# Start of the split-weight buffers inside a 128-byte line, in a two-block transformer kernel on one core

## The chip, the cores and the metric

The kernel runs on one core of one Trainium2 chip. The metric is the device time of one execution in microseconds, and a kernel is told by the median of its runs.

## The reference

Two blocks of two layers each are computed for one sequence of 256 tokens with 1024 features, in float32. The first block mixes a gated linear recurrence with latent attention and then sends every token to two of sixteen experts; the second has a gated recurrence, a chunked attention and wide MLPs. What takes the time is matrix products with weights that are each used once:

```
proj = h @ w_in                                   # 1024 x 4768, per layer of block 1
he = jax.nn.silu(t @ w_gate[e]) * (t @ w_up[e])   # 16 experts, 1024 x 512
y = y + combine[:, e:e + 1] * (he @ w_down[e])
z = hn @ w_in                                     # block 2, recurrence, 1024 x 2816
sqrelu_mlp: jnp.square(jax.nn.relu(hn @ w1)) @ w2 # 1024 x 4096 x 1024, twice
```

## The kernel before

Activations lie with features on the 128 partitions and the 256 tokens along the free dimension. Weights arrive in pieces of 1 MB (128 partitions x 2048 floats) in a ring of five buffers `raw`, loaded by SyncE's queue in the order in which `weights()` (L399) is called. `parts_of()` (L429) splits each half of a piece, 1024 floats in a partition, into a rounded part and a rest: ScalarE writes `whi` (L444), VectorE subtracts and writes `wlo` (L445). The pool `wsp` has three buffers of each, taken in turn by the counter `turn`; the recurrent layer adds two more of each (pool `wse`, `EXTRA`).

Each product in float32 is then made of three matmuls in `mm3()` (L456): high by high (L459), low by high (L460) and high by low (L461). Every matmul has a stationary operand, which a weight load (PEld) brings into the array, and a moving operand, which streams through it. The names of a matmul in the trace stand as out<-moving,stationary.

- In linears (`linear_gen`, L475) a slice of 128 columns of `whi` or `wlo` is stationary, 512 bytes in a partition, and the activations move, 256 tokens, 1024 bytes. The tiles are `h_hi`/`h_lo`, `a_hi`/`a_lo` (the MLP's hidden layer), `xc`, `mg`, `oa`, `ob`, `hq`, `oo`.
- In token-major linears (`linear_tok_gen`, L529; the values of the first block, keys and values of the second) a slice of `h` is stationary and 256 columns of `whi`/`wlo` move.
- In the experts (`project` and `down` in `moe`) a slice of `xg` or `hT` is stationary and 512 columns of `whi`/`wlo` move.

The scheduling is by program order on each engine, with semaphores between them. [...]

The layout that the program is built with: `whi` begins at 101632, 105728 and 109824 bytes in a partition, `wlo` at 113920, 118016 and 122112. All six are multiples of 128, and a slice's start adds a multiple of 512. `h_hi` begins at 44224, `h_lo` at 52416, `xc_hi` and `a_hi` at 134720, that is, at 64 past a multiple of 128; `xg`, `hT` and the other expert tiles begin at multiples of 128. Small unused tiles (`shift`) put them there. The attention's probabilities `p`, which are stationary in the transposes of L1179, begin at 32 or 96 past a multiple of 128 in the mixers and at 0 or 64 past one in the second block's attention.

The one place outside the weights where an operand begins off such a boundary is the convolution of the recurrent layer (L1601), which reads `xr[:, j:j + T]` for j = 1, 2, 3, at 4, 8 and 12 bytes past a tile's start.

Of the kernel before, what the change touches and what calls it, by code (L numbers as in the profile page):

```python
# [9 lines left out]
F32R = mybir.dt.float32r  # L10
# [7 lines left out]
D, T, P = 1024, 256, 128  # L18
# [4 lines left out]
CONV = 1024  # L23
# [159 lines left out]
def program(tc, A, out, dbg=None):  # L183
    nc = tc.nc
    from contextlib import ExitStack, nullcontext
    with ExitStack() as st:
# [217 lines left out]
        def weights(ap, nk, nn):  # L404

            if READY and not OWN:
                return READY.pop(0)
            raw = PRE.pop(0) if PRE and not OWN else None
            if raw is None:
                raw = OWN[0].tile([P, RING], F32, tag="own", name="own") if OWN else room()  # L410
                with tc.issue_after(LOADS[0].ins) if LOADS else nullcontext():
                    nc.sync.dma_start(raw[:, :nk * nn], ap[:, :nk * nn])
            if GATE:
                with ExitStack() as es:
                    for g in GATE.pop():
                        es.enter_context(tc.issue_after(g.ins))
                    return parts_of(raw, nk, nn)
            return parts_of(raw, nk, nn)

        EXTRA, turn = [None, 0], [-1]  # L420
# [5 lines left out]

        DEFER = []

        def parts_of(raw, nk, nn):  # L429
            per_ = max(1, CONV // nn)  # L430
            parts = []
            for k0 in range(0, nk, per_):
                n = min(per_, nk - k0) * nn
                src = raw[k0 // per_] if isinstance(raw, list) else raw[:, k0 * nn:k0 * nn + n]
                if OWN:
                    hl = (OWN[1].tile([P, 2, CONV], F32R, tag="e0", name="own_w") if k0 == 0 else
                          OWN[2].tile([P, 2, CONV], F32R, tag="cn", name="own_w"))
                    hi, lo = hl[:, 0], hl[:, 1]
                else:
                    turn[0] = (turn[0] + 1) % (3 + EXTRA[1])  # L440
                    p_ = wsp if turn[0] < 3 else EXTRA[0]
                    hi = p_.tile([P, CONV], F32R, tag="whi", name="whi")
                    lo = p_.tile([P, CONV], F32R, tag="wlo", name="wlo")
                nc.scalar.copy(hi[:, :n], src)  # L444
                low = lambda lo=lo, hi=hi, src=src, n=n: nc.vector.tensor_sub(lo[:, :n], src, hi[:, :n].bitcast(F32))  # L445
                if k0 and DEFER:
                    DEFER.append(low)
                else:
                    low()
                parts.append((hi, lo))  # L450

            def w(k, c, n):
                i, o = k // per_, k % per_ * nn + c
                return [t[:, o:o + n] for t in parts[i]]
            return w
# [336 lines left out]
        def first_linear(pcs, nxt, mw, mx, ma, evac):  # L792
# [42 lines left out]
            for i, raw in enumerate(raws):  # L835
                w = parts_of(raw, 8, 2 * P)
                ps = bank(("hg", "at")[i // 2], "ps_f").rearrange("p (c t) -> p c t", c=2)
                pss += [ps[:, 0], ps[:, 1]]
                for n, (k, c) in enumerate([(k, c) for k in range(8) for c in range(2)] if i == 0 else
                                           [(k, c) for c in range(2) for k in range(8)]):  # L840
                    wh, wl = w(k, c * P, P)
                    nc.tensor.matmul(ps[:, c], wh, y[0][:, k, :], start=n == 0, stop=False, skip_group_check=True)
                    nc.tensor.matmul(ps[:, c], wh, y[1][k], start=False, stop=False, skip_group_check=True)
                    nc.tensor.matmul(ps[:, c], wl, y[0][:, k, :], start=False, stop=k == 7, skip_group_check=True)
                    if n % 8 == 7:
                        m = 2 * i + n // 8
                        ada_fill(SHIFT[m])
                        if m == SHIFT_DONE[0]:
                            shift_done()
                        if m == SHIFT_DONE[1]:  # L850
                            shift_products()
                        if m == NEXT:
                            ready(nxt)
# [1047 lines left out]
```

## Time and profile before

| | us |
|---|---|
| runs: median, lowest, highest of 3 | 1828.7, 1824.86, 1834.02 |
| profiled execution, its own time | 1828.03 |
| span of its instructions | 1826.3 |
| TensorE busy (matmul) in the span | 1750.9 |
| VectorE busy | 1465.8 |
| ScalarE busy | 1130.6 |

The profiled execution lies 0.7 us below the median; 1.7 us of its time lie outside the span. In the stretches named below, 58 to 285 us and 605 to 860 us are the mixers of the first block's layers, 285 to 605 us and 860 to 1168 us their experts, 1168 to 1306 us the recurrent layer, 1306 to 1500 us the first MLP, 1500 to 1650 us the attention and 1650 to 1826 us the second MLP. Matmuls are pipelined, so the length that the profile gives one (280 ns) is longer than the distance to the next; where a stream runs without a wait, its pace is read from the starts.

### The profile page before, as it was taken

The numbers are of one execution on the slowest core, as the hardware profiler recorded it, in microseconds if no ns is written. First come the engines' busy times: TensorE is split into PE (matmuls) and PEld (weight loads), VectorE is DVE, ScalarE is ACT, GpSimd is POOL, SyncE is SP. The second block draws the span as 40 slices with busy tenths as digits, with TensorE's granted clock in tenths as the row PEclk, the third lists the DMA queues.
The fourth block names the chain that finished last, engine by engine and source line by source line (L and its number), as shares of the span: only waits on it lengthen the run. The fifth ranks groups of instructions, "written<-read, shape, count | busy, mean of one in ns | idle before, by whom it ended". The sixth has DMA issues, their size and how long they took to land. (4 is left out here: it accounts for less than half of the span.)

```text
span 1826.3 us, 31669 instructions
## 1 busy us (share of the span) xinstructions
PE 1750.9 (96%) x12430; PEld 1551.3 (85%) x12430; DVE 1465.8 (80%) x2514; ACT 1130.6 (62%) x1758; POOL 39.2 (2%) x40
## 2 busy tenths in 40 slices
PE   7999998999999899998999999999999999999999
PEld 5887897888878797897888887798899998889999
DVE  4887897999998677898998999797897666667754
ACT  3754546877777556545877777578555446546642
POOL 0000000000000000000000000000000002100000
PEclk9999998999999899999999999899999999999999
DMA  9565797797999456688697899657687764456552
GB/s 352 216 246 226 275 347 283 283 347 278 353 344 344 146 209 251 245 323 346 250 345 303 326 354 357 236 203 262 215 323 280 273 248 148 173 189 258 203 194 85
DMA packets 71727, 485.62 MB, mean 266 GB/s; under 512 B 8720, under 2 KB 10896, under 8 KB 14352
## 3 DMA queue, kind: packets, MB, share of 16 engines
q1 hardware_dynamic: 70992, 483.21, 71.0%
q8 instruction: 101, 1.65, 0.4%
q14 instruction: 58, 0.48, 0.1%
q10 hardware_dynamic: 576, 0.27, 0.1%
HBM read 482.41 MB, written 1.05 MB: 265 GB/s over the span
## 5 line engine op out<-in xcount | busy, mean ns | idle before, releaser
L445 DVE TENSOR_TENSOR wlo<-raw,whi 128x1024 fp32r<-128x1024 f32 (+1 forms) x628 | 752.9, 1210 | 151.7 <-ACT whi L444 136.6
L444 ACT CAST whi<-raw 128x1024 fp32r<-128x1024 f32 (+1 forms) x628 | 649.8, 1041 | 272.8 <-PE ps_mm L460 162.7
L459 PE MATMUL ps_mm<-h_hi,whi 128*128 128x256 f32 x1168 | 330.5, 286 | 6.8 <-ACT h_hi L656 4.2
L461 PE MATMUL ps_mm<-h_hi,wlo 128*128 128x256 f32 x1168 | 328.1, 283 | 1.5 <-DVE wlo L445 1.4
L460 PE MATMUL ps_mm<-h_lo,whi 128*128 128x256 f32 x1168 | 329.1, 283 | 0.0
L459 PEld LDWEIGHTS ps_mm<-h_hi,whi 128*128 128x128 f32 x1168 | 222.5, 192 | 12.6 <-ACT h_hi L656 5.9
L461 PEld LDWEIGHTS ps_mm<-h_hi,wlo 128*128 128x128 f32 x1168 | 222.7, 191 | 4.8 <-DVE wlo L445 3.7
L460 PEld LDWEIGHTS ps_mm<-h_lo,whi 128*128 128x128 f32 x1168 | 223.1, 191 | 2.1 <-issue 1.4
L460 PE MATMUL ps_e<-wlo,xg 128*128 128x512 f32 x512 | 202.4, 395 | 2.6 <-DVE wlo L445 2.3
L459 PE MATMUL ps_e<-whi,xg 128*128 128x512 f32 x512 | 202.7, 396 | 1.2 <-ACT whi L444 1.1
L461 PE MATMUL ps_e<-whi,xg 128*128 128x512 f32 x512 | 200.2, 391 | 0.0
L459 PE MATMUL ps_mm<-a_hi,whi 128*128 128x256 f32 x512 | 142.4, 278 | 0.0
L461 PE MATMUL ps_mm<-a_hi,wlo 128*128 128x256 f32 x512 | 142.1, 278 | 0.0
L460 PE MATMUL ps_mm<-a_lo,whi 128*128 128x256 f32 x512 | 142.1, 278 | 0.0
L305 DVE SCALAR_TENSOR_TENSOR raw<-raw,cb 128x1024 f32<-128x1024 f32 x112 | 135.6, 1216 | 1.5 <-DMA raw<-in_ada_dram 1.4
L460 PEld LDWEIGHTS ps_e<-wlo,xg 128*128 128x128 f32 x512 | 96.2, 188 | 26.8 <-DVE wlo L445 8.5
L459 PEld LDWEIGHTS ps_e<-whi,xg 128*128 128x128 f32 x512 | 96.2, 188 | 20.8 <-ACT whi L444 1.9
L461 PEld LDWEIGHTS ps_e<-whi,xg 128*128 128x128 f32 x512 | 96.1, 188 | 18.6
L460 PE MATMUL py<-wlo,hT 128*128 128x512 f32 x256 | 101.0, 394 | 0.0
L461 PE MATMUL py<-whi,hT 128*128 128x512 f32 x256 | 99.8, 390 | 0.0
L459 PE MATMUL py<-whi,hT 128*128 128x512 f32 x256 | 99.2, 390 | 0.0
L461 PEld LDWEIGHTS ps_mm<-a_hi,wlo 128*128 128x128 f32 x512 | 96.2, 188 | 0.0
(694 smaller groups left out, 3476.5 us busy)
## 6 DMA issues: line engine op xcount, KB each, us to landing
raw<-in_ada_dram SPq DMA_DIRECT2D x104, 1024.0 KB, 5.9
raw<-in_mw_dram SPq DMA_DIRECT2D x64, 1024.0 KB, 4.9
raw<-in_w_up_dram SPq DMA_DIRECT2D x56, 1024.0 KB, 4.9
raw<-in_w_down_dram SPq DMA_DIRECT2D x56, 1024.0 KB, 4.9
raw<-in_w_gate_dram SPq DMA_DIRECT2D x44, 1024.0 KB, 4.8
raw<-in_win_dram SPq DMA_DIRECT2D x34, 1024.0 KB, 5.0
more<-in_w_gate_dram SPq DMA_DIRECT2D x12, 1024.0 KB, 5.1
raw<-in_lwin_dram SPq DMA_DIRECT2D x11, 1024.0 KB, 5.9
```

Source lines behind the costliest of these rows:

```text
L305: nc.vector.scalar_tensor_tensor(w, w, 1.0, cb, op0=OP.mult, op1=OP.mult, accum_out=mod[:, m:m + 1])
L444: nc.scalar.copy(hi[:, :n], src)
L445: low = lambda lo=lo, hi=hi, src=src, n=n: nc.vector.tensor_sub(lo[:, :n], src, hi[:, :n].bitcast(F32))
L459: nc.tensor.matmul(ps, ah, bh, start=start, stop=False)
L460: nc.tensor.matmul(ps, ah, bl, start=False, stop=False)
L461: nc.tensor.matmul(ps, al, bh, start=False, stop=stop)
```

## The change

Every buffer of `whi` and `wlo` is made 128 bytes longer, and 4096 of its 4224 bytes are used, from a start that depends on the buffer: 30, 31 or 2 floats (120, 124 or 8 bytes) where the piece is not 512 columns wide, and 0 where it is.

```diff
+        LINE = (30, 31, 2)
+
         def parts_of(raw, nk, nn):
...
                     p_ = wsp if turn[0] < 3 else EXTRA[0]
-                    hi = p_.tile([P, CONV], F32R, tag="whi", name="whi")
-                    lo = p_.tile([P, CONV], F32R, tag="wlo", name="wlo")
+                    o = LINE[turn[0] % 3] if nn != 512 else 0
+                    hi = p_.tile([P, CONV + 32], F32R, tag="whi", name="whi")[:, o:o + CONV]
+                    lo = p_.tile([P, CONV + 32], F32R, tag="wlo", name="wlo")[:, o:o + CONV]
```

The instructions, their order on every engine and their waits are the same in both programs. Of the matmuls of `mm3`, 6150 of 256 columns get a stationary operand that begins at 120, 124 or 8 past a multiple of 128, and 576 of 256 columns (and 24 of 512) such a moving operand. The 2304 of the experts, and 384 of the mixers' output projections, whose pieces are 512 columns wide too, keep multiples of 128. All tiles behind `wsp` move by 768 bytes, six times 128; `h_hi`, `h_lo` and the ring stay. The six buffers now lie 4224 bytes apart instead of 4096.

## Rows read from the trace of the kernel before

**Rows 1.** Page, part 1: the span and TensorE's busy time.

```profile
span 1826.3 us, 31669 instructions
...
PE 1750.9 (96%) x12430; PEld 1551.3 (85%) x12430; DVE 1465.8 (80%) x2514; ACT 1130.6 (62%) x1758; POOL 39.2 (2%) x40
```

**Rows 2.** Stretches: a mixer, experts, recurrent layer, attention; engines' busy us (instructions), clock, DMA.

```profile
58.00:285.00 227.00, 220.07 (x1745) 195.81 (x1743) 192.51 (x487) 126.68 (x259) 5.91 (x6) 0.98 0.71 267
285.00:605.00 320.00, 306.35 (x1440) 251.67 (x1441) 287.73 (x343) 239.95 (x275) 2.31 (x2) 0.97 0.83 312
1168.00:1306.00 138.00, 131.15 (x1170) 120.80 (x1163) 117.19 (x205) 96.78 (x162) 0.70 (x1) 0.99 0.67 246
1500.00:1650.00 150.00, 143.86 (x1223) 123.68 (x1223) 99.04 (x243) 85.50 (x204) 19.54 (x17) 0.99 0.48 180
```

**Rows 3.** Stretches of 100 us inside the two MLPs, columns as in rows 2.

```profile
1385.00:1485.00 100.00, 100.00 (x852) 100.00 (x851) 66.77 (x92) 43.38 (x54) 0.00 (x0) 1.00 0.73 267
1655.00:1755.00 100.00, 100.00 (x885) 100.00 (x884) 69.23 (x102) 58.41 (x99) 0.00 (x0) 1.00 0.57 197
```

**Rows 4.** Timeline of PE: first and last matmul followed 116 to 119 ns later.

```profile
58.79 0.28 PE L459 MATMUL ps_mt<-whi,h_hi 128*128 128x256 f32 x1
...
1653.94 0.28 PE L461 MATMUL ps_mm<-h_hi,wlo 128*128 128x256 f32 x1
```

**Rows 5.** Timeline of PE: first and last matmul followed 113 to 115 ns later.

```profile
69.89 0.28 PE L460 MATMUL ps_mt<-wlo,h_hi 128*128 128x256 f32 x1
...
1822.13 0.28 PE L460 MATMUL ps_mm<-a_lo,whi 128*128 128x256 f32 x1
```

**Rows 6.** Timeline of PE, experts: start, length, line, out<-moving,stationary; nine matmuls from first to last.

```profile
472.24 0.39 PE L461 MATMUL ps_e<-whi,xg 128*128 128x512 f32 x1
...
474.28 0.39 PE L461 MATMUL ps_e<-whi,xg 128*128 128x512 f32 x1
```

**Rows 7.** Groups of the page, part 5: the two halves of the split.

```profile
L445 DVE TENSOR_TENSOR wlo<-raw,whi 128x1024 fp32r<-128x1024 f32 (+1 forms) x628 | 752.9, 1210 | 151.7 <-ACT whi L444 136.6
L444 ACT CAST whi<-raw 128x1024 fp32r<-128x1024 f32 (+1 forms) x628 | 649.8, 1041 | 272.8 <-PE ps_mm L460 162.7
```

**Rows 8.** Groups by form on VectorE: 256 floats read at odd starts, and at even ones.

```profile
L1601 DVE SCALAR_TENSOR_TENSOR y<-xr,c_cols,y 128x256 f32<-128x256 f32 x33 | 14.8, 479 | 0.0
...
L654 DVE SCALAR_TENSOR_TENSOR nt<-xT,gain,rs 128x256 f32<-128x256 f32 x16 | 7.1, 479 | 1.7 <-ACT rs L1759 1.7
```

**Rows 9.** Timeline of PE: four transposes of `p` in a mixer and four in the attention.

```profile
203.51 0.60 PE L1179 MATMUL ps_pt<-c_ident,p 128*128 128x128 f32 x4
...
1599.55 0.60 PE L1179 MATMUL ps_pt<-c_ident,p 128*128 128x128 f32 x4
```

**Rows 10.** Timeline of PE, first MLP: two stretches of nine matmuls around a short gap.

```profile
1366.13 0.28 PE L459 MATMUL ps_mm<-h_hi,whi 128*128 128x256 f32 x1
...
1367.19 0.28 PE L459 MATMUL ps_mm<-h_hi,whi 128*128 128x256 f32 x1
...
1367.43 0.32 PE L461 MATMUL ps_mm<-h_hi,wlo 128*128 128x256 f32 x1
1367.58 0.28 PE L459 MATMUL ps_mm<-h_hi,whi 128*128 128x256 f32 x1
...
1367.93 0.28 PE L459 MATMUL ps_mm<-h_hi,whi 128*128 128x256 f32 x1
...
1368.95 0.28 PE L459 MATMUL ps_mm<-h_hi,whi 128*128 128x256 f32 x1
```

**Rows 11.** Timeline of PE, recurrent layer: six matmuls before and after a new moving tile.

```profile
1228.17 0.28 PE L459 MATMUL ps_mm<-h_hi,whi 128*128 128x256 f32 x1
...
1228.85 0.28 PE L459 MATMUL ps_bd<-xc_hi,whi 128*128 128x256 f32 x1
...
1229.56 0.28 PE L459 MATMUL ps_bd<-xc_hi,whi 128*128 128x256 f32 x1
```

## The prediction

> **What bounds the kernel now.** The profiled execution took 1828.03 us, 0.7 below the median of 1828.7, and its instructions span 1826.3; the sum below is made against 1828.0. I read the page's busy times first: TensorE is busy 1750.9 us of the span, 96%, VectorE 80% and ScalarE 62% [rows 1]. By stretch it is no different: 220 of 227 us in a mixer, 306 of 320 in the experts, 131 of 138 in the recurrent layer, 144 of 150 in the attention [rows 2]. So time is won or lost in the pace at which matmuls follow each other.
>
> That pace is the second thing to read. [...] Among the 6922 pairs of matmuls of `mm3` with 256 columns that follow each other in the whole trace, 3289 are 116 to 119 ns apart [rows 4], 3211 are 113 to 115 ns apart [rows 5], and 422 are further apart or wait. Of the slow ones 1142 lie in the first MLP, 1 in the second, 1096 in the two mixers, 433 in the recurrent layer, 615 in the attention and 2 in the experts' stretches. In the experts' quiet stretches nine matmuls of 512 columns take 2.04 us, 226.7 ns each, which is the fast level for twice the columns [rows 6].
>
> **What the change does, part by part.** It moves no instruction and no wait; it moves addresses. Four things could cost or give.
>
> The writers. ScalarE's and VectorE's split, 1.04 and 1.21 us [rows 7], now write to starts 8 or 12 bytes past a multiple of 16. The nearest rows are the convolution's 33 operations, which read 256 floats at 4, 8 and 12 bytes past a tile's start: 479 ns, the same as 16 operations of that form at even starts [rows 8]. I take 0. Were each of the 628 a per cent slower, VectorE would lose 7.5 us in all, and in the linears, where the odd starts are, it is idle for a third of the time (67 us busy of 100 in the first MLP [rows 3]); so the bounds on the path are 0 and 7.5 us.
>
> The weight load by itself. A slice of 512 bytes that starts at 120, 124 or 8 lies in one 128-byte line more than before. The nearest rows are the transposes, whose stationary `p` starts at 32 or 96 past a multiple of 128 in the mixers, and at 0 or 64 past one in the attention: four of them take 0.60 us in both places [rows 9]. Those starts are still multiples of 32, so this says little of 8 and 124, but a load by itself shows no price. I take 0, with the slow level as the upper bound (below).
>
> The pace. This is the term. What is it that tells a fast stream from a slow one? The level holds for hundreds of matmuls and survives from slice to slice and buffer to buffer. In this layout all buffers look alike to TensorE, since all of them, and all slices, start at a multiple of 128. It changes where the stream is disturbed: in the first MLP nine matmuls take 1.06 us (117.8 ns), then one comes 0.15 us after its predecessor instead of 0.12, and soon nine take 1.02 us (113.3) [rows 10]. And once it changes with no wait at all, at the place where the moving tile goes from `h` to `xc`, another address: six matmuls take 0.68 us before it and 0.71 after [rows 11]. I read this as two streams, the load of the next weights and the running matmul, which go through their lines of memory side by side; in one relation of phase they get into each other's way by 4.4 ns in a matmul, in the other they don't, and the relation lasts until something shifts it. A start that is one or two floats away from the boundary shifts the load's crossings against the matmul's; and since the three buffers have three different starts, the relation is set anew every 8 slices (24 matmuls), so that a slow stretch of 850 matmuls at one phase [rows 3] is no longer possible. 6150 matmuls get such a start. My forecast is that the linears then run at the fast level nearly everywhere.
>
> The price, if they do: the first MLP gives 1142 x 4.4 ns = 5.0 us, all on the path, as TensorE has no idle time there. Mixers, recurrent layer and attention hold 1096 + 433 + 615 = 2144 slow pairs, 9.4 us; VectorE is busy 193 of 227 us in a mixer and 117 of 138 in the recurrent layer [rows 2], so part of what TensorE gains there it will spend waiting for the split, and I count four fifths, 7.5 us. Together 12.5 us: 1828.0 - 12.5 = 1815.5, I say 1816. Its own range is 1811 (some of the experts' uneven stretches profit too) to 1822 (half of it).
>
> The experts. They keep multiples of 128, at the fast level for the most part [rows 6]. But the buffers lie 4224 apart instead of 4096, so two of three change by 128 against a multiple of 256, and the change of pace in [rows 11] was between two tiles that are both 64 past a multiple of 128. Bounds: 0, and 2304 x 8.8 ns = 20 us lost if all of them fell to the slow level. I take 0, as nothing else here points to 256, and put the bound into the range.
>
> [...]
>
> **The rivals.** First, no change: the level is set by the moment at which a stream restarts after a wait, whatever the addresses are. For it speaks that both levels occur at the same starts, thousands of times each [rows 4, 5], and that the change of pace comes with a gap [rows 10]; against it [rows 11], where no gap is. Then the shares stay as they are, with the luck of the two MLPs: one that turns slow costs 1510 x 4.4 = 6.6 us, one that turns fast gives 5.0. That is 1828, between 1822 and 1835, which is also about how far the three runs lie apart.
>
> Second, slower: the line that each shifted load touches in addition is one more place for the two streams to meet, and it is there in every phase. The nearest price for a meeting is the slow level itself: if the 3211 fast pairs become slow, 3211 x 4.4 = 14 us are lost, four fifths to all of it on the path, 1839 to 1842. It decides against the change from 9.1 us on, that is, 1.5 ns in each of the 6150 shifted matmuls. For it speaks that the starts before are all multiples of 32, the second MLP runs 1510 pairs at the fast level with them, and none starts in the middle of 16 bytes; against it that a load at 32 or 96 shows no price [rows 9]. [...]
>
> Third, a larger gain: with no meeting of any kind the pace could fall to that of the transposes, of which four take 0.60 us with the 0.28 that the last one lasts, 0.11 us from start to start [rows 9, 10]. Some 4 ns below the fast level on 6150 matmuls are 25 us more, 1791. Nothing in 6500 pairs of linears lies below 113 ns, so this gets little.
>
> **How the numbers follow.** Forecast (fast level) 46%, no change 30%, slower 19%, larger gain 5%. A measurement of this kernel tells a difference from none at about 0.5%, 9.1 us. Of the forecast's 46 about 40 end beyond that, with the larger gain 45; of the slower rival's 19 and the unlucky end of no change 22 in all; 33 stay within. The range must hold forecast and no change, 1811 to 1835; it reaches a little further on both sides, 1808 to 1838, and leaves out the larger gain and most of the slower rival, 5 and 13%.
>
> **What would show it.** In the profile after: the two stretches of 100 us in the MLPs both with 880 matmuls or more, and the pairs at 116 to 119 ns reduced from 3289 to some hundreds; the split still 1.04 and 1.21 us; the experts' nine matmuls still in 2.04 us. The forecast is wrong if both levels keep their shares (the first rival), if the share at 113 to 115 shrinks or a third, slower level appears (the second), or if the pace improves and the time doesn't, in which case VectorE's split has become what TensorE waits for.

## The result, and the profile after

The changed kernel takes 1844.34 us, the median of its runs (1841.75 to 1846.5), against 1826.88 for the kernel before, measured beside it: a ratio of 1.0082 with a 95% interval of 1.006 to 1.0104. It is slower; forecast were 1816 us and a range up to 1838. The profiled execution took 1844.61 us. The page after, part 1, answers to [rows 1]; TensorE has gained 21 us of busy time, the other engines next to nothing:

```profile
span 1842.8 us, 31669 instructions
...
PE 1772.0 (96%) x12430; PEld 1568.1 (85%) x12430; DVE 1468.4 (80%) x2514; ACT 1130.4 (61%) x1758; POOL 39.2 (2%) x40
```

The lines of the code lie four further: `mm3` at L463 to L465, the split at L448 and L449. The split groups (page, part 5, as [rows 7]) cost what they did, at starts inside 16 bytes too:

```profile
L449 DVE TENSOR_TENSOR wlo<-raw,whi 128x1024 fp32r<-128x1024 f32 (+1 forms) x628 | 754.0, 1210 | 160.9 <-ACT whi L448 156.9
L448 ACT CAST whi<-raw 128x1024 fp32r<-128x1024 f32 (+1 forms) x628 | 649.6, 1040 | 286.4 <-PE ps_mm L464 171.1
```

Stretches after, columns as in [rows 2]: the first layer's experts, and 100 us in each MLP, as far from the MLP's first matmul as in [rows 3]:

```profile
284.00:607.00 323.00, 311.27 (x1439) 253.68 (x1439) 289.04 (x343) 239.54 (x275) 2.30 (x2) 0.96 0.82 309
...
1393.00:1493.00 100.00, 100.00 (x849) 100.00 (x848) 67.46 (x92) 43.25 (x55) 0.00 (x0) 1.00 0.74 268
1664.00:1764.00 100.00, 100.00 (x846) 100.00 (x845) 66.74 (x100) 56.70 (x98) 0.00 (x0) 1.00 0.54 191
```

Neither MLP runs at 880 or more: the second fell from 885 to 846 matmuls in 100 us at the same clock, and the first stayed where it was. The two levels of before (113.3 and 117.8 ns) are gone: taken 24 at a time (as many as one buffer serves), those of the second MLP with h moving have means of 117.8 to 119.4 ns, where each group had 113.3 before. A timeline of PE there (start, length, line) has 24 matmuls from the first to the last row in 2.85 us, 118.8 ns each; single distances differ (0.13, then 0.11):

```profile
1699.73 0.28 PE L463 MATMUL ps_mm<-h_hi,whi 128*128 128x256 f32 x1
...
1701.15 0.28 PE L463 MATMUL ps_mm<-h_hi,whi 128*128 128x256 f32 x1
1701.28 0.28 PE L464 MATMUL ps_mm<-h_lo,whi 128*128 128x256 f32 x1
1701.39 0.28 PE L465 MATMUL ps_mm<-h_hi,wlo 128*128 128x256 f32 x1
...
1702.58 0.28 PE L463 MATMUL ps_mm<-h_hi,whi 128*128 128x256 f32 x1
```

The experts became slower too: 21 matmuls in 4.86 us, 231.4 ns, where [rows 6] have 226.7 (timeline of PE):

```profile
474.14 0.39 PE L463 MATMUL ps_e<-whi,xg 128*128 128x512 f32 x1
...
479.00 0.39 PE L463 MATMUL ps_e<-whi,xg 128*128 128x512 f32 x1
```

Where the 16.5 us of span lie is read by taking the same matmul of TensorE's order in both traces as a stage's border. The table starts at TensorE's first matmul, which comes 0.8 us later than before. The first column is worked out so from the traces of before and after, the others in the same way for the first four experiments, always against before:

| us longer than before | after | e1 | e2 | e3 | e4 |
|---|---|---|---|---|---|
| start and mixer 0 | -1.9 | -5.4 | -3.2 | -0.4 | -1.5 |
| experts 0 | 3.2 | 3.6 | 0.0 | 0.0 | -0.4 |
| mixer 1 | 2.4 | 0.9 | 1.8 | 3.0 | 6.6 |
| experts 1 | 3.0 | 3.7 | -0.3 | -0.2 | 0.0 |
| recurrent layer | 0.9 | -0.2 | 0.7 | 0.9 | -0.6 |
| MLP 0 | 0.7 | -4.6 | 0.5 | 0.3 | -0.7 |
| attention | -0.1 | -0.9 | 0.3 | 0.3 | -0.6 |
| MLP 1 | 7.6 | 0.0 | 7.6 | 6.2 | 0.0 |

Of the after column 6.1 us are the experts', whose pieces were not shifted inside their buffers, and 9.6 the rest's. Each column is one profiled execution. How far that can be off shows in e4, which by its median is as fast as before, and has 6.6 us more in mixer 1.

### The profile page after: what moved, and what is told of

Same layout as the page of the kernel before. It is cut to its first block, busy times and chain, and to the rows that moved or that the text cites. A ratio compares the mean times of both kernels' runs of the same rounds, so it can differ in the third digit from the quotient of the medians.

```text
span 1842.8 us, 31669 instructions
## 1 busy us (share of the span) xinstructions
PE 1772.0 (96%) x12430; PEld 1568.1 (85%) x12430; DVE 1468.4 (80%) x2514; ACT 1130.4 (61%) x1758; POOL 39.2 (2%) x40
## 5 line engine op out<-in xcount | busy, mean ns | idle before, releaser
L449 DVE TENSOR_TENSOR wlo<-raw,whi 128x1024 fp32r<-128x1024 f32 (+1 forms) x628 | 754.0, 1210 | 160.9 <-ACT whi L448 156.9
L448 ACT CAST whi<-raw 128x1024 fp32r<-128x1024 f32 (+1 forms) x628 | 649.6, 1040 | 286.4 <-PE ps_mm L464 171.1
L463 PE MATMUL ps_mm<-h_hi,whi 128*128 128x256 f32 x1168 | 333.2, 288 | 6.7 <-ACT h_hi L660 4.2
L465 PE MATMUL ps_mm<-h_hi,wlo 128*128 128x256 f32 x1168 | 331.0, 285 | 1.6 <-DVE wlo L449 1.3
L463 PEld LDWEIGHTS ps_mm<-h_hi,whi 128*128 128x128 f32 x1168 | 222.3, 192 | 12.7 <-ACT h_hi L660 6.0
L465 PEld LDWEIGHTS ps_mm<-h_hi,wlo 128*128 128x128 f32 x1168 | 222.0, 191 | 4.2 <-DVE wlo L449 3.1
L463 PE MATMUL ps_e<-whi,xg 128*128 128x512 f32 x512 | 204.3, 399 | 1.1 <-ACT whi L448 1.0
L465 PE MATMUL ps_e<-whi,xg 128*128 128x512 f32 x512 | 201.0, 393 | 0.0
L463 PE MATMUL ps_mm<-a_hi,whi 128*128 128x256 f32 x512 | 144.2, 282 | 0.0
L465 PE MATMUL ps_mm<-a_hi,wlo 128*128 128x256 f32 x512 | 143.9, 281 | 0.0
L463 PEld LDWEIGHTS ps_e<-whi,xg 128*128 128x128 f32 x512 | 96.3, 188 | 22.7 <-ACT whi L448 1.8
L465 PEld LDWEIGHTS ps_e<-whi,xg 128*128 128x128 f32 x512 | 96.2, 188 | 20.1
L465 PE MATMUL py<-whi,hT 128*128 128x512 f32 x256 | 100.4, 392 | 0.0
L463 PE MATMUL py<-whi,hT 128*128 128x512 f32 x256 | 100.3, 394 | 0.0
L464 PEld LDWEIGHTS ps_mm<-a_lo,whi 128*128 128x128 f32 x512 | 96.8, 189 | 0.0
```

The source lines that it names most:

```text
L463: nc.tensor.matmul(ps, ah, bh, start=start, stop=False)
L464: nc.tensor.matmul(ps, ah, bl, start=False, stop=False)
L465: nc.tensor.matmul(ps, al, bh, start=False, stop=stop)
```

## The experiments

In all tables and texts "pairs" are the 6922 of [rows 4, 5]: fast 113 to 115 ns, slow 116 to 119, other anything else (before: 3211, 3289, 422, of which 343 are over 130 ns apart). The groups are bins for single distances: a pace that is steady but lies between the bins or above them counts as "other", or in part as each.

**Theory and rival.** The theory after the result: the odd starts slow the linears, and the buffers' distance of 4224 (16.5 times 256) slows the experts. The rival: one of the two does it all.

**First four: starts and distance apart.** e1 keeps the distance and takes the starts away; e2 keeps the starts and makes the distance 4352, 17 times 256; e3 has one odd start instead of three; e4 is the control with distance 4352 and no odd start. Against the changed kernel:

```diff
# e1
-                    o = LINE[turn[0] % 3] if nn != 512 else 0
+                    o = 0
# e2, e3, e4: 64 floats of padding in wsp, 32 in wse
+                    pad = 64 if turn[0] < 3 else 32
-                    hi = p_.tile([P, CONV + 32], F32R, tag="whi", name="whi")[:, o:o + CONV]
+                    hi = p_.tile([P, CONV + pad], F32R, tag="whi", name="whi")[:, o:o + CONV]
...
# e3
+                    o = 2 if nn != 512 else 0
# e4
+                    o = 0
```

> Only the buffers' length is changed (4224 bytes apart), every slice still starts at a multiple of 128. Theory A, the odd starts cost: the time stays at that of before, about 1827, with two sharp levels (113 and 118 ns) in the linears and 226.7 ns in the experts. Theory B, the distance of 4224 costs, because whi and wlo no longer agree against a multiple of 256: 1838 to 1845, the experts' matmuls lose the 226.7 ns level as in the changed kernel, and the second MLP has no sharp level.

> The odd starts 120, 124 and 8 as in the change, but the six main buffers lie 4352 bytes apart, 17 times 256. Theory A: the linears' pace stays spread around 118 ns and the time is about 1838 (the experts, with no odd start, are back at 226.7 ns). Theory B: about 1827 and sharp levels in the linears.

> One odd start for all buffers in the linears, 8 bytes past a multiple of 128, buffers 4352 apart. Theory A: slower than before by about as much as with three different starts, about 1838. If it is the difference between the three starts that breaks the sharp levels, not the odd start: about 1827 or less, with sharp levels. Theory B: about 1827.

> All starts at multiples of 128, buffers 4352 bytes apart: the control for the two above. Theories A and B both expect the time of before, about 1827. If it is as slow as the changed kernel, then it is the distance as such (against 512 or more) or the place of the tiles behind the buffers that costs.

| run | us | ratio, interval | fast, slow, other |
|---|---|---|---|
| e1 | 1826.36 | 1.0002, 0.9983 to 1.002 | 5070, 1154, 698 |
| e2 | 1837.77 | 1.008, 1.0052 to 1.0108 | 997, 3633, 2292 |
| e3 | 1837.74 | 1.0075, 1.0049 to 1.0102 | 810, 3609, 2503 |
| e4 | 1826.03 | 0.9998, 0.9981 to 1.0015 | 3503, 2987, 432 |
| after | 1844.34 | 1.0082, 1.006 to 1.0104 | 812, 3886, 2224 |

Starts cost 1837.77 - 1826.03 = 11.7 us, one start as much as three. The remaining 1844.34 - 1837.77 = 6.6 us go with the distance. The times alone don't show that, as the intervals of e2 and after overlap nearly whole; the table of stages does: the experts take 3.0 to 3.7 us more a layer in both kernels with 4224, 6.1 in all in the changed one, and at most 0.4 more or less in the three with 4352. e1's equality hides two effects: its experts lose 7.3 us, and the rest, where 5070 pairs are fast, wins 10.2 in this profile; by the medians the two cancel. So the gain that was forecast exists in part, but it came with the distance, not with the starts. Stretches of the two MLPs, first of e1, then e2, then e4:

```profile
1385.00:1485.00 100.00, 100.00 (x884) 99.96 (x883) 70.16 (x96) 45.74 (x58) 0.00 (x0) 1.00 0.74 274
1665.00:1765.00 100.00, 100.00 (x884) 100.00 (x884) 64.71 (x92) 55.24 (x89) 0.00 (x0) 1.00 0.56 199
```

```profile
1385.00:1485.00 100.00, 100.00 (x847) 100.00 (x846) 66.26 (x89) 44.37 (x55) 0.00 (x0) 1.00 0.71 262
1665.00:1765.00 100.00, 100.00 (x848) 100.00 (x847) 64.47 (x93) 53.34 (x89) 0.00 (x0) 1.00 0.53 186
```

```profile
1385.00:1485.00 100.00, 99.38 (x844) 99.14 (x843) 68.93 (x95) 44.44 (x57) 0.00 (x0) 1.00 0.73 268
1665.00:1765.00 100.00, 100.00 (x884) 100.00 (x884) 66.22 (x97) 56.50 (x92) 0.00 (x0) 1.00 0.56 197
```

The experts in e1 and in e2 (timeline of PE): 12 matmuls in 2.77 us, 230.8 ns, with the distance 4224, and 11 in 2.50 us, 227.3 ns, with 4352:

```profile
473.76 0.39 PE L463 MATMUL ps_e<-whi,xg 128*128 128x512 f32 x1
...
476.53 0.39 PE L463 MATMUL ps_e<-whi,xg 128*128 128x512 f32 x1
```

```profile
473.62 0.39 PE L461 MATMUL ps_e<-whi,xg 128*128 128x512 f32 x1
...
476.12 0.39 PE L463 MATMUL ps_e<-whi,xg 128*128 128x512 f32 x1
```

**Is e1's gain in the linears real?** e5 to e7 give the linears the differences of 128 that the distance 4224 made, and leave the experts alone (all from e4; `oh` and `ol` are the starts of `whi` and `wlo` in floats):

```diff
# e5: as with distance 4224
+                    oh, ol = ((0, 32, 0)[turn[0] % 3], (32, 0, 32)[turn[0] % 3]) if nn != 512 else (0, 0)
# e6: only whi against wlo
+                    oh, ol = (0, 32) if nn != 512 else (0, 0)
# e7: only buffer against buffer
+                    oh, ol = ((0, 32, 0)[turn[0] % 3], (0, 32, 0)[turn[0] % 3]) if nn != 512 else (0, 0)
```

> Buffers 4352 bytes apart (17 x 256). Experts at starts that are alike against 256 bytes, as before the change. Linears: the high part's three buffers start at 0, 128 and 0, the low part's at 128, 0 and 128 against a multiple of 256, which repeats for the linears alone what the kernel with buffers 4224 apart had. Theory (a start that is a multiple of 128 but differs by 128 between successive stationary operands favours the fast level in the linears and costs only in the experts): experts' layers within 0.5 us of before, over 4800 of the 6922 pairs at 113 to 115 ns, time 1826 - 9 = 1817 us, 1815 to 1820. Rival (the fast share in the kernel 4224 apart was luck of the moments at which the stream restarted): fast share anywhere between 3000 and 4000, time 1822 to 1829 us.

> Only the low part starts 128 bytes further, in every buffer of the linears; buffers 4352 apart. If it is the difference between the high and the low part that makes the fast level likelier: over 4800 fast pairs and 1817 us. If it is the difference from buffer to buffer: shares as before, about 3200 to 3500 fast pairs, 1824 to 1828 us.

> High and low part start alike, but the second of the three buffers 128 bytes further; buffers 4352 apart. If the difference from buffer to buffer is what makes the fast level likelier: over 4800 fast pairs and 1817 us. If it is the difference between high and low part: shares as before and 1824 to 1828 us. If both count in part, 1820 to 1824 us in this kernel and in the one with the low part moved.

| run | us | ratio, interval | fast, slow, other |
|---|---|---|---|
| e5 | 1819.93 | 0.9972, 0.9957 to 0.9988 | 5065, 1141, 716 |
| e6 | 1821.73 | 0.9977, 0.996 to 0.9994 | 4226, 1922, 774 |
| e7 | 1818.93 | 0.9967, 0.9952 to 0.9983 | 4658, 1819, 445 |

e5's 5065 fast pairs match e1's 5070, and its experts are as before (-0.3 and -1.3 us). Against 1825.23 for the kernel before, measured beside them, the gain is 5.3, 3.5 and 6.3 us, so both differences count, and not in sum. In the pairs e6 and e7 fall between their alternatives; in time e6 lies where both differences counting in part was to put it (1820 to 1824 us), e7 below that. All three beat both kernels; these runs don't tell e5 and e7 apart, and one of them is the version to keep.

**Which starts are bad?** The others, all at distance 4352 (the recurrent layer's two more buffers, in `wse`, stay at 4224). e8 and e9 move all weights of the linears by 64 and by 16 bytes (e4 with `oh, ol = (16, 16)` and `(4, 4)`). e11, e12 and e13 are e8, e4 and e7 with the moving tile h 64 bytes further (the ring `raw`, which `mm3` does not read, moves with it):

```diff
# e11 to e13
-        hp = pool("hp", 1)
+        hp = pool("hp", 1); hp.tile([P, 16], F32, tag="sh0", name="sh0", bufs=1)
-        shift(pool("sh0", 1), 64, "sh0")
```

e14, e16, e17 and e18 have weights and h moved together, by 2, 8, 4 and 0 floats (K below); both halves of h lie in one tile there, and e18 is the control for that:

```diff
-            hi = hp.tile([P, 8, T], F32R, tag="h_hi", name="h_hi")
-            lo = hp.tile([P, 8, T], F32R, tag="h_lo", name="h_lo")
+            hh = hp.tile([P, 16 * T + 8], F32R, tag="h", name="h")
+            hi, lo = [hh[:, K + i:K + i + 8 * T].rearrange("p (k t) -> p k t", t=T) for i in (0, 8 * T)]
...
-        shift(pool("sh0", 1), 64, "sh0")
+        shift(pool("sh0", 1), 32, "sh0")
```

> All buffers of the linears start 64 bytes past a multiple of 128, 4352 apart. If a slice must begin at a multiple of 128 to stay at the two sharp levels (one line of 128 bytes more touched is what costs): spread pace, mean about 118 ns, 1826 + 11.7 = 1838 us. If a multiple of 64 or less is enough: two sharp levels, 1822 to 1829 us.

> Buffers 4352 apart, the weights of the linears at 64 past a multiple of 128, and the moving tile h moved by 64 bytes to a multiple of 128; the other moving tiles (xc, the MLP's hidden layer a, mg, hq, oo) stay at 64. Theory A (a slice of 512 bytes that does not begin at a multiple of 128 costs by itself): the pace is spread everywhere, time 1838 to 1841 us. Theory B (what counts is the distance of the two operands' starts against 128 bytes; half a line apart is good): linears with h at two sharp levels as in the kernel before, only those with a and the others spread, which are about half, time 1831 to 1834 us.

> Buffers 4352 apart, weights at multiples of 128, h at a multiple of 128 instead of 64 past one. Theory A (the weights' start alone counts): two sharp levels, 1822 to 1829 us. Theory B (distance of the two starts): linears with h spread, 1831 to 1834 us, while the second halves of the MLPs, where a moves, keep the sharp levels.

> As the kernel whose second buffer starts 128 bytes further for high and low part (1819 us), but with h at a multiple of 128. Theory A: 1817 to 1822 us, pace at 113 to 115 ns in over 4600 pairs. Theory B: linears with h spread, 1826 to 1830 us.

> Buffers 4352 apart, every weight slice of the linears at 8 past a multiple of 128 (as in the kernel that took 1837.7 us), and the moving tile h at 72 past one instead of 64, so that the two starts are 64 apart again, at an odd place. Theory A (a start that is no multiple of 16 or of 128 costs by itself): linears with h stay spread at a mean of 118 ns or more, time 1836 to 1840 us. Theory B (only the distance of the two starts against 128 bytes counts): linears with h return to the sharp levels of 113 to 115 and 116 to 119 ns with less than 100 of some 3400 pairs in between or above, and those with other moving tiles stay spread; time 1828 to 1833 us.

> As the kernel with weights at 8 and h at 72 (1846.15 us), but weights at 32 and h at 96 past a multiple of 128: half a line apart, both at multiples of 32. Theory C (two conditions: starts half of 128 bytes apart, and no start inside 32 bytes or less): linears with h at the sharp levels, mean below 116 ns, those with a, mg, hq, oo and xc (32 apart) spread or slow, time 1829 to 1835 us. Theory D (a start must be a multiple of 64, at any distance): linears with h spread at 118 ns or more, 1838 to 1847 us.

> The same with weights at 16 and h at 80. Theory C with 16 bytes as the unit: linears with h sharp, mean below 116 ns, 1829 to 1836 us. Theory C with 32 as the unit, or theory D: spread at 118 ns or more, 1838 to 1847 us.

> The control of the two others and of the kernel with weights at 8 and h at 72: the same single tile for both halves of h and the same places of everything else, with weights at 0 and h at 64. If nothing but the starts matters in these kernels: sharp levels and 1822 to 1830 us. If the single tile or the ring, which lies 32 bytes further, costs something: 1832 us or more, and the three others are to be read against this one.

> The kernel with all weight buffers of the linears at 8 past a multiple of 128 (1837.7 us), with 8 changed to 16 and nothing else; h and the other moving tiles stay at 64, so the distance is 48 instead of 56. If a start inside 16 bytes is what costs: two sharp levels, in the linears with h and with a, fewer than 150 of 6922 pairs between or above them without a wait, 1822 to 1829 us. If the half line of distance is what counts, so that 48 is no better than 56: spread, mean 118 ns, 1834 to 1838 us.

Starts are bytes past a multiple of 128; the two ns columns are means from start to start over the pairs up to 130 ns, of 3418 with h moving and 1534 with the MLP's a moving (a is always at 64). They are of one profiled execution, the us of all runs; the two lie up to 5.7 us apart (e16: 1825.06 in the profile):

| run | weights, h | ns with h, with a | us | ratio, interval |
|---|---|---|---|---|
| before | 0, 64 | 115.0, 115.6 | | |
| e18 | 0, 64 | 115.0, 115.6 | 1827.37 | 0.9995, 0.9982 to 1.0008 |
| e17 | 16, 80 | 114.0, 116.7 | 1826.11 | 0.9986, 0.9972 to 0.9999 |
| e16 | 32, 96 | 114.7, 116.7 | 1830.77 | 1.0015, 0.9998 to 1.0033 |
| e9 | 16, 64 | 118.6, 116.7 | 1835.29 | 1.0044, 1.0028 to 1.006 |
| e3 | 8, 64 | 118.3, 117.2 | 1837.74 | 1.0075, 1.0049 to 1.0102 |
| e14 | 8, 72 | 120.6, 120.0 | 1846.15 | 1.0092, 1.0057 to 1.0127 |
| e8 | 64, 64 | 118.7, 120.0 | 1840.46 | 1.0094, 1.0068 to 1.012 |
| e11 | 64, 0 | 114.5, 120.0 | 1832.51 | 1.0036, 1.0017 to 1.0054 |
| e12 | 0, 0 | 119.7, 117.8 | 1836.59 | 1.005, 1.0031 to 1.0068 |
| e13 | 0 or 128, 0 | 119.2, 113.5 | 1829.11 | 1.0032, 1.0013 to 1.005 |

The page's stretches show it without means. In the second MLP h moves between 1660 and 1720 us, and a between 1745 and 1805; a fast stretch of 60 us holds 531 or 532 matmuls, a slow one 512. First e4 and e15 (below), whose linears start alike, at 0 with h at 64; then e8, then e11, where of these matmuls' operands only h has moved, then e12, where the weights are back at 0:

```profile
1660.00:1720.00 60.00, 60.00 (x531) 60.00 (x531) 43.96 (x68) 37.44 (x67) 0.00 (x0) 1.00 0.56 197
1745.00:1805.00 60.00, 60.00 (x531) 60.00 (x531) 29.36 (x29) 23.11 (x22) 0.00 (x0) 1.00 0.54 187
```

```profile
1660.00:1720.00 60.00, 60.00 (x512) 60.00 (x511) 42.16 (x64) 36.43 (x64) 0.00 (x0) 1.00 0.53 189
1745.00:1805.00 60.00, 60.00 (x512) 60.00 (x512) 27.65 (x26) 22.79 (x22) 0.00 (x0) 1.00 0.53 184
```

```profile
1660.00:1720.00 60.00, 60.00 (x508) 60.00 (x507) 42.28 (x66) 36.20 (x64) 0.00 (x0) 1.00 0.53 191
1745.00:1805.00 60.00, 60.00 (x502) 60.00 (x502) 26.51 (x25) 21.73 (x22) 0.00 (x0) 1.00 0.58 199
```

```profile
1660.00:1720.00 60.00, 60.00 (x532) 60.00 (x531) 43.65 (x67) 37.32 (x67) 0.00 (x0) 1.00 0.57 194
1745.00:1805.00 60.00, 60.00 (x502) 60.00 (x501) 27.02 (x27) 21.20 (x21) 0.00 (x0) 1.00 0.48 170
```

```profile
1660.00:1720.00 60.00, 60.00 (x502) 60.00 (x501) 42.14 (x66) 36.45 (x65) 0.00 (x0) 1.00 0.54 192
1745.00:1805.00 60.00, 60.00 (x511) 60.00 (x511) 28.81 (x29) 22.62 (x23) 0.00 (x0) 1.00 0.55 190
```

e4 and e15 set the scale: at the same starts the whole second MLP can be at either level, so a mean between 113.3 and 117.8 ns, or a share of fast pairs in one profile, says little by itself. What tells starts apart is a pace that is neither level.

Theory B held for e11 and e12 in where the two levels occur: weights at 64 are bad when h is there too (118.7 ns, e8) and good when h is 64 away (114.5, e11), and h at 0 is good or bad by where the weights are (114.5 with them at 64, e11; 119.7 with them at 0, e12). So neither 0 nor 64 is bad by itself; the pair is. But the bad pace is not spread, as the expectations had it. With both operands at the same place it is a steady 120.0 ns with a in e8 and e11 (502 matmuls in 60 us) and with h in e12 (502; all 31 groups of 24 in the second MLP take 120.0), but not with h in e8 (508, a mean of 118.7). e12 took 3 us more than B gave it; in its profile, the longest of its runs (1841.29), the MLPs' second halves are at the slow level nearly whole (1532 of 1534 pairs), which these starts allow. e13 came as B expected in its time; h is at 119.2, a at 113.5.

Then the same stretches of e3, e14, e17 and e9, for e14 with 70 us of a in the first MLP ahead of them:

```profile
1660.00:1720.00 60.00, 60.00 (x509) 60.00 (x508) 42.48 (x66) 35.98 (x66) 0.00 (x0) 1.00 0.55 193
1745.00:1805.00 60.00, 60.00 (x516) 60.00 (x516) 27.50 (x27) 22.85 (x23) 0.00 (x0) 1.00 0.56 202
```

```profile
1410.00:1480.00 70.00, 70.00 (x570) 70.00 (x569) 44.77 (x58) 27.79 (x30) 0.00 (x0) 1.00 0.69 254
1660.00:1720.00 60.00, 60.00 (x499) 60.00 (x499) 43.08 (x68) 36.53 (x65) 0.00 (x0) 1.00 0.57 212
1745.00:1805.00 60.00, 60.00 (x516) 60.00 (x515) 30.25 (x33) 23.93 (x27) 0.00 (x0) 1.00 0.55 193
```

```profile
1660.00:1720.00 60.00, 60.00 (x532) 60.00 (x531) 43.80 (x67) 37.33 (x67) 0.00 (x0) 1.00 0.55 194
1745.00:1805.00 60.00, 60.00 (x516) 60.00 (x516) 28.09 (x27) 23.06 (x22) 0.00 (x0) 1.00 0.48 170
```

```profile
1660.00:1720.00 60.00, 60.00 (x508) 60.00 (x507) 41.72 (x65) 35.57 (x64) 0.00 (x0) 1.00 0.54 192
1745.00:1805.00 60.00, 60.00 (x517) 60.00 (x516) 27.79 (x26) 21.88 (x21) 0.00 (x0) 1.00 0.54 187
```

In e14 theory B fell: the distance is 64 again, but at 8 and 72 the linears with h are slower than ever, and the time is beyond theory A's 1840 too. e17 and e16 have the same distance at multiples of 16 and keep the two levels with h, and in e18 the single tile costs nothing (1827.37 us, 0.9995). So at this distance the start at 8, inside 16 bytes, costs (120.6 ns with h in e14 against 114.0 in e17 and 114.7 in e16); whether it is the weights' or h's, e14 doesn't tell. Not all of what e14 takes beyond e3 (8.4 us by the medians, 5.4 with each set against the kernel before beside it) is h's: a, at 8 and 64 in both, runs at 123.3 ns in e14's first MLP (570 in 70 us) and at 117.8 in e3's, which is 767 x 5.5 = 4.2 us, and at 116.7 in the second MLP of both. One pair of starts has shown three paces, and what picks one is not known.

e9 met neither expectation. 8 changed to 16 alone leaves h at 118.6 (118.3 in e3), with 1238 pairs above 119 ns. With a the pairs lie at 115 to 118 ns, which fills the bins but is no return to the two levels: it is a steady 116.7 (516 or 517 in 60 us), as with a in e16, e17 and e3's second MLP. By the medians, each against the kernel before beside it, e9 keeps 8.2 of e3's 11.7 us, by the ratios 0.44 of 0.75%; the two intervals overlap. So more than half of what the start at 8 costs is there at 16 too, and a start inside 16 bytes need not be the main reason. In e9 both moving tiles lie at 64 against 128 bytes, but h lies at 192 against 256, a at 64, and their paces differ. If it is the address that makes the difference, the distance that counts is not one against 128 bytes alone; what counts instead stays open.

**The experts, and the sum of the good places.** e15 is e4 with the experts' pieces (and the mixers' output projections) at 64; e19 is e17 with e5's differences in `wsp`:

```diff
# e15
+                    oh, ol = (16, 16) if nn == 512 else (0, 0)
# e19
+                    oh, ol = ((4, 36, 4)[turn[0] % 3], (36, 4, 36)[turn[0] % 3]) if nn != 512 else (0, 0); oh, ol = (oh, ol) if turn[0] < 3 or nn == 512 else (4, 4)
```

> Buffers 4352 apart, linears at multiples of 128 as before; the pieces that are 512 columns wide (experts, mixers' output projections) start 64 bytes further, so that the experts' moving weights lie half a line from their stationary tiles xg and hT, which are at multiples of 128. Theory B1 (half a line apart is good whichever operand is the weight): the experts' layers at most as long as before, possibly shorter, time 1822 to 1828 us. Theory B2 (it depends on the roles; in the experts equal starts are the good place): each experts' layer 3 to 8 us longer, time 1832 to 1842 us. The output projections, 384 matmuls, lose up to 2 us in both.

> The two things together that gave most fast pairs: weights at 16 and h at 80 (82% of the pairs with h fast), and the high and the low part's buffers 128 bytes apart against 256 as in the kernel of 1819.9 us. If both help independently: over 5000 fast pairs and 1815 to 1819 us. If the share of the fast level is set by the 128 bytes alone: 1818 to 1822 us, no gain over that kernel.

e15: 1832.01 us, 1.0007 (0.9987 to 1.0027). The two experts' layers take 1.7 and 0.0 us longer, between the theories; of some 1110 pairs of 512 columns in each layer 824 and 795 were at 228 ns or below in e4, 321 and 313 are in e15. 64 bytes apart is no gain there, and a small loss. Its linears start as e4's, but only 1748 of their pairs are fast (3503 in e4), and the second MLP alone takes 6.6 us more, so its time says little of the experts. e19: 1832.96 us, 1.0027 (1.0017 to 1.0038), 1420 fast pairs, 1702 other: the two good things together are bad. Against 256 bytes its distances, 64 and 192, are those of e5, so a rule of one distance fails here too.

## Why the prediction was wrong

**The step that failed is "The pace".** It read two streams that get into each other's way in one relation of phase; the phase was the author's reading, and no run shows it. The 4.4 ns a matmul come from [rows 3]: less three matmuls each that had begun before the stretch, the two counts give 117.8 and 113.4 ns from start to start. That the pace hangs on a relation between addresses of both operands is now shown: 64 bytes of h alone move it between the two levels of before and a pace that is neither (118.7 ns in e8 against 114.5 in e11, 119.7 in e12 against 114.7 in e4). What failed is the conclusion that a shift off the boundary, set anew every 24 matmuls, frees the stream from the slow level. None of the new relations is a free one: in the second MLP with h the groups of 24 take 117.8 to 119.4 ns after the change, 118.0 to 118.5 in e2, and with one start at 8 (e3) all 31 take 118.3. In every experiment with starts at 8, or at 120, 124 and 8, the linears' means lie at 117 to 121 ns, about the slow level or above it. Over all pairs the mean went from 115.65 to 118.27 ns, 2.6 ns, beyond the 1.5 ns from which the second rival was to decide. That rival had the right direction and 1839 to 1842 us for it; e2 and e3, which hold this cost alone, took 1838.

**The second rival's reason is at most half right.** It named a 128-byte line more for each load; that the memory has lines of that length was assumed, and no run shows it. In e16 and e17 every slice reaches past one more multiple of 128 too, and the linears with h keep the levels (114.7 and 114.0 ns). Its point that no start before lay in the middle of 16 bytes is what e14 against e16 and e17 supports (120.6 ns at 8, 114.0 at 16, 114.7 at 32). That does not say why h is at 118.6 in e9, where no start lies inside 16 bytes, nor why e12, where h and the weights start at multiples of 128, is at 119.7. So what made the linears slow in the change itself is shown to be the starts; by which rule stays open.

The first rival, by which addresses do not count, fails as far as pace goes: moving h by 64 bytes, with the weights where they were, made each matmul 5.0 ns slower in the mean (e4 to e12) or 4.2 faster (e8 to e11). The loads themselves stayed as long (188 ns in the profile, for a's weights in before, after and e2 alike).

**The experts' term was mis-sized.** Bounds were 0 and 20 us, and 0 was taken; it is 6.1. The change of pace in [rows 11], between two tiles that differ by 128 against 256, was seen as a hint at it and given nothing all the same. Without this term the result would have been at the edge of the range.

**The cover was misjudged, as far as one profile tells.** Four fifths of the mixers', recurrent layer's and attention's pace was to count. Over all stages the pairs became 2.6 ns x 6600 = 17 us slower. Of these 7.4 us lie in the mixers, the recurrent layer and the attention, which grew by 1.4 us in all (the table, with the start), and 9.9 in the MLPs, which grew by 8.2. In the attention 1.0 us of slower pace cost nothing (-0.1). The 1.4 is uncertain by some 4 us, since the same stages take 3.8 us more in e4, whose starts are those of before. So most of the price is paid in the MLPs, where TensorE has next to no idle time (busy 100.00 us of 100 in the two stretches after).

**What was right:** the writers (1.21 and 1.04 us as before), and the load by itself (its 188 ns, and e16 and e17). The second MLP's 6.6 us, written for a level that turns slow by luck, came near its 7.6, but the starts made it, not luck. The first MLP, mostly slow before, had little to lose. The third rival's floor was misread: the transposes of [rows 9] move 128 columns, not 256, so their 0.11 us says nothing of the pace of a linear.

**Open** are the rule by which the starts decide, which part of the cost at 8 a start inside 16 bytes has, why differences of 128 between successive weights help at multiples of 128 (e5 to e7) and hurt at 16 (e19), and what picks the level within a run at starts that allow several. Not tried were starts at 4 or 12, and moving operands of other lengths.

## What to carry to other kernels

Where TensorE streams short matmuls back to back, count matmuls in equal stretches of a quiet stage before and after a change of layout: no wait showed the change of pace here (885 matmuls in 100 us before and 846 after, with TensorE busy for all of them at a granted clock of 1.00). 113.3 and 117.8 ns both occur at the same starts (e4 and e15), so one profile's share of them says little; 116.7, 118.3, 118.7, 120.0 and more were seen only with other starts. Starts at 8 were not at the fast level here with h (118.3 ns in e3, 120.6 in e14), and a multiple of 16 was not enough (118.6 in e9). Try a few placements for each kind of product, as the linears were bad with both operands at the same place of 128 bytes (118.7 to 120.0 ns in e8, e11 and e12) and the experts were better there than 64 bytes off it (824 and 795 of some 1110 pairs at 228 ns or below in e4, 321 and 313 in e15), and as single good placements didn't add up (e5 1819.93 us, e17 1826.11, both together in e19 1832.96). A padding changes every buffer's distance: give it a size that leaves the buffers alike for those users that were fast, here 256 bytes (at most 0.4 us more or less for an experts' layer, e2 to e4) and not 128 (3.0 to 3.7 us more, e1 and after), and change starts and distances in runs of their own.

## What was not expected of the hardware

A moving tile's place alone changes the pace: 64 bytes of h took its linears from 114.7 ns (e4) to 119.7 (e12). Other starts have steady paces of their own: 120.0 ns with both operands at the same place (a in e8, 1520 of 1534 pairs above 119 ns; a in e11; h in e12), 116.7 with a in e9 and e17, 118.3 with h in e3, 123.3 with a in e14's first MLP. Not all places are so even: h in e8, at the same place as its weights, has a mean of 118.7. And 128 bytes between buffers, with every start still a multiple of 128, cost the experts 3.0 to 3.7 us a layer (226.7 to 231.4 ns, before to after), while they give the linears 3.5 to 6.3 us (e5 to e7).
